# Modulation rows, scratch fills and small weights of later use ordered behind the opening's last modulation row; two more row buffers in the first feed-forward

## The chip, the cores and the metric

The kernel runs on one core of a Trainium2 chip. The metric is the device time of one execution in microseconds (us); a kernel's time is the median of its runs. TensorE (PE) multiplies matrices into PSUM banks, VectorE (DVE) and ScalarE (ACT) work element by element, GpSimd (POOL) does the rest, and SyncE (SP) issues nearly all DMAs of this kernel, in one queue and in the order in which they stand in it. Each engine works through its instructions in order; semaphores make one wait for another.

## What is computed

A decoder trunk of two layers in float32: 256 tokens, model width 2048, feed-forward width 5632. In each layer a vector of 6 x 2048 modulation values comes from the conditioning vector:

```python
cond = jax.nn.silu(c)
for l in range(DEPTH):
    mod = (jnp.einsum('bd,de->be', cond, w_ada[l]) + b_ada[l]).reshape(B, N_MOD, 1, D_MODEL)
    sh_m, sc_m, gt_m, sh_f, sc_f, gt_f = [mod[:, i] for i in range(N_MOD)]
    u = x * (1 + sc_m) + sh_m
    proj = u @ w_in[l]
    ...
    mix = jnp.concatenate([y_attn, y_rwkv], axis=-1) @ w_out[l]
    x = layer_norm(DEEPNORM_ALPHA * x + gt_m * mix, ln1_w[l], ln1_b[l])
    u = x * (1 + sc_f) + sh_f
    gate, up = jnp.split(u @ w_gate_up[l], 2, axis=-1)
    ffn = (jax.nn.silu(gate) * up) @ w_down[l]
    x = layer_norm(DEEPNORM_ALPHA * x + gt_f * ffn, ln2_w[l], ln2_b[l])
```

`y_attn` is sliding-window attention over part of the projected columns and `y_rwkv` a linear recurrence with data-dependent decay over the others. The modulation weights alone are 2 x 2048 x 12288 values, about 200 MB, of which every value is used once.

## The kernel before, in words

**Planning.** The program is written in the order of the mathematics; a planner then fixes the order of the instructions on each engine ahead of time, by a simulated timeline and by the order in which they were written. A tile comes from a pool by a tag with a number of buffers; an instruction that writes a tile waits until the earlier user of that buffer is done. `tc.add_manual_dep(a, b, order, ...)` adds an edge without a semaphore: on their common queue `a` is put behind `b`.

**Modulation rows.** One row is a tile `ast` of 128 x 1024 values, 512 KB of `w_ada`. DVE multiplies row j by the conditioning value `cond[:, j]` and adds it to `aacc`. After 16 rows TensorE transposes the sums, ACT adds them up and DVE writes them to `mods`.

**The opening** (`ada_first`, lines 340 to 356, called by `parts`, line 1354) needs the first two modulation vectors of layer 0 before anything can be projected. It goes by column parts of 4, 4, 4, 2 and 2 blocks of 128 columns (`PARTS`), with eight row buffers, and behind each part the input projection of these columns runs (`front`). Lines 351 and 353 are DVE's sums, line 322 the transposes. `lead` holds the name of the last modulation row's DMA issued so far (line 348). Line 1374 lays later parameter rows behind it through `setup`. Then follow `rope` and the two fills of the DRAM scratch `tinv` with zeros (line 1381), which the inversion in the recurrence later writes partly over (line 790).

**All other modulation values** come in units of 1024 columns, 16 rows each, by `ada_steps` (line 251), which runs as a side stream: `pump` (line 378) advances it by `pace` steps per weight tile. Its rows (line 261) have two buffers in the pool `adap`. The first product is line 263, the other sums line 265, and these are laid behind the weight stream by `anchor`. In part of the mixer of layer 0 the flag `direct` sends rows through TensorE instead (`ada_direct`).

**Weights** are fetched by `steps` (line 414): a raw tile of 128 x 1024 with four buffers (line 422), which ACT rounds to a high part `hi` (line 430) and DVE subtracts to a low part `lo` (line 431). `stream` and `tstream` multiply both parts (lines 452 to 455 and 464 to 466).

**Decays** (line 640) loads for each group of heads two small weights into the tile `w2a2` (lines 644 and 645).

**The feed-forward** in `channel` (line 1180, pool `fp`) goes over eleven blocks of 512 gate and 512 up columns, in two groups of six and five, each group followed by the down projection of its rows. Line 1283 is the gate's activation, line 1329 the end of a down projection's block.

Of the kernel before, what the change touches and what calls it, by code (L numbers as in the profile page):

```python
# [10 lines left out]
F32 = mybir.dt.float32  # L11
# [8 lines left out]
P = 128  # L20
# [49 lines left out]
def hybrid_trunk_kernel(  # L70
# [9 lines left out]
    dma = nc.sync.dma_start  # L80
# [4 lines left out]
    adap = ctx.enter_context(tc.tile_pool(name="adap", bufs=1))  # L85
# [6 lines left out]
    def bank(name="mb", tag="mb"):  # L92

        if tag == "cb":
            return ps.tile([P, 512], F32, tag="cb", name=name)
        t = f"m{turn[0]}"
        turn[0] ^= turn[1]
        return ps.tile([P, 512], F32, tag=t, name=name, bufs=1)
# [49 lines left out]
    order = mybir.DependencyInfo(mybir.DependencyClass.NoSync, mybir.DependencyReason.DATA)  # L148
# [20 lines left out]
    def drv(l, nm, i, n=1):  # L169
        return der[l][:, DO[nm] + i:DO[nm] + i + n]  # L170

    def setup(sp, l, half, behind=None):

        prow = sp.tile([P, P], F32, tag="prow", bufs=2, name=f"prow{l}{half}")
        G.memset(prow, 0.0)
        lst = [[("b_ada", b_ada[l], 96), ("ln1_w", ln1_w[l], 16), ("ln1_b", ln1_b[l], 16)],
               [("ln2_w", ln2_w[l], 16), ("ln2_b", ln2_b[l], 16), ("w0", rwkv_w0[l], 8),
                ("a0", rwkv_a0[l], 8), ("k_k", rwkv_k_k[l], 8), ("k_a", rwkv_k_a[l], 8),
                ("r_k", rwkv_r_k[l].rearrange("h d -> (h d)"), 8), ("gn_w", rwkv_gn_w[l], 8),
                ("gn_b", rwkv_gn_b[l], 8), ("mu", rwkv_mu[l, 0:26 * P], 26)]][half]  # L180

        def load(dst, src):
            ins = dma(dst, src)
            if behind:
                tc.add_manual_dep(ins.ins, behind[0], order, reason="behind the first modulation rows")

        r = 0
        for nm, src, n in lst:
            load(prow[r:r + n], src.rearrange("(r q) -> r q", q=P))
            PC[nm] = half * P + r  # L190
            r += n
            yield
        if half:
            load(prow[r:r + 1, 0:32], rwkv_mu[l:l + 1, 26 * P:26 * P + 32])
            r += 1
            PC["v0"] = P + r
            if l > 0:
                load(prow[r:r + 8], rwkv_v0[l - 1].rearrange("(r q) -> r q", q=P))
            load(nsink[l], attn_sinks[l:l + 1, :].to_broadcast([P, 16]))
            V.tensor_scalar_mul(nsink[l], nsink[l], -1.0)  # L200
            yield
        pt = bank()
        PE.transpose(pt[:, 0:P], prow, ident)
        V.tensor_copy(par[l][:, half, :], pt[:, 0:P])
        if half:
            V.tensor_scalar(drv(l, "omu", 0, 27), prm(l, "mu", 0, 27), -1.0, 1.0, ALU.mult, ALU.add)
            V.tensor_scalar_mul(drv(l, "w0h", 0, 8), prm(l, "w0", 0, 8), 0.5)
            V.tensor_scalar_mul(drv(l, "a0h", 0, 8), prm(l, "a0", 0, 8), 0.5)
            V.tensor_scalar_mul(drv(l, "kah", 0, 8), prm(l, "k_a", 0, 8), 0.5)
            V.tensor_scalar(drv(l, "okah", 0, 8), prm(l, "k_a", 0, 8), -0.5, 1.0, ALU.mult, ALU.add)  # L210
            V.tensor_scalar_mul(drv(l, "kkh", 0, 8), prm(l, "k_k", 0, 8), -0.5)
            V.tensor_scalar_mul(drv(l, "v0h", 0, 8), prm(l, "v0", 0, 8), 0.5)
# [38 lines left out]
    def ada_steps(l, mod, c0):  # L251

        src = w_ada[l].rearrange("(j p) n -> p j n", p=P)
        n0 = mod * D + c0
        if direct[0]:
            yield from ada_direct(l, mod, c0, src[:, :, n0:n0 + 1024])
            return
        acc = adap.tile([P, 1024], F32, tag="aacc", name="aacc")
        for j in range(KT):
            t = adap.tile([P, 1024], F32, tag="ast", name="ast", bufs=2)  # L260
            dma(t, src[:, j, n0:n0 + 1024])
            if j == 0:
                V.tensor_scalar_mul(acc, t, cond[:, 0:1])
            else:
                ins = V.scalar_tensor_tensor(acc, t, cond[:, j:j + 1], acc, ALU.mult, ALU.add)  # L265
                if anchor:
                    tc.add_manual_dep(ins.ins, anchor[0], order, reason="behind the weight stream")
            yield
        for _ in range(LAG):
            yield  # L270

        ada_sums(l, mod, c0, [acc[:, i * P:(i + 1) * P] for i in range(8)])
        done.add((l, mod, c0 // 1024))
        yield
# [63 lines left out]
    lead = []  # L338
# [19 lines left out]
    done = set()  # L358
# [14 lines left out]
                       + halves(1, 5))  # L373
    pace = [0.0, 0.0]
    anchor = []
    direct = [False]

    def pump():

# [160 lines left out]
    def mixer(l, us, mixp, feeds):  # L540
# [33 lines left out]
        if l > 0:  # L574
# [7 lines left out]
            for p2 in range(4):  # L582
# [3 lines left out]
                for i in range(2):  # L586
                    p = 2 * p2 + i
                    PE.matmul(b[:, i * T:(i + 1) * T], lhsT=v2t[64:96, i * P:(i + 1) * P], rhs=hv, start=True, stop=True)
                for i in range(2):
                    p = 2 * p2 + i  # L590
# [49 lines left out]
        def decays(g):  # L640

            gsl = slice(g * T, (g + 1) * T)
            w2a2 = pa.tile([P, T], F32, tag="w2a2", name="w2a2", bufs=1)
            dma(w2a2[0:64, :], rwkv_w2[l, :, gsl])
            dma(w2a2[64:128, :], rwkv_a2[l, :, gsl])
            zb, ab = bank("zb"), bank("ab")
            for i in I2:
                PE.matmul(zb[:, i * T:(i + 1) * T], lhsT=w2a2[0:64, i * P:(i + 1) * P], rhs=twd[0:64, :], start=True, stop=True)
                PE.matmul(ab[:, i * T:(i + 1) * T], lhsT=w2a2[64:128, i * P:(i + 1) * P], rhs=xwa[64:128, :],
                          start=True, stop=True)  # L650
            st = [dict(p=2 * g + i) for i in I2]
            for i in I2:
                s_, p = st[i], 2 * g + i
                lw = pa.tile([P, T], F32, tag="t_lw", name="lw", bufs=2)
                S.activation(lw, zb[:, i * T:(i + 1) * T], AF.Tanh, scale=0.5, bias=drv(l, "w0h", p))
                s_["tha"] = tha = pa.tile([P, T], F32, tag="t_tha", name="tha", bufs=4)
                S.activation(tha, ab[:, i * T:(i + 1) * T], AF.Tanh, scale=0.5, bias=drv(l, "a0h", p))
                V.tensor_scalar(lw, lw, -0.5 * DECAY, -0.5 * DECAY, ALU.mult, ALU.add)
                V.tensor_tensor_scan(lw, rmask, lw, 0.0, ALU.mult, ALU.add)
                s_["e1"] = e1 = pa.tile([P, NCH, CH + 1], F32, tag="e1", name="e1", bufs=4)  # L660
                V.memset(e1[:, :, 0:1], 1.0)
                S.activation(e1[:, :, 1:CH + 1], lw.rearrange("p (c s) -> p c s", s=CH), AF.Exp)
                s_["el"] = el = pb.tile([P, NCH, 1], F32, tag="el", name="el", bufs=4)
                S.activation(el, lw.rearrange("p (c s) -> p c s", s=CH)[:, :, CH - 1:CH], AF.Exp)
                s_["e2"] = e2 = pa.tile([P, T], F32, tag="t_e2", name="e2", bufs=4)
                S.activation(e2, lw, AF.Exp, scale=-1.0)
            vt_ = bank("vt")
            if g == 0:
                warm(vt_, IDLE["dec"][l])
            for cc in range(NCH):  # L670
                for i in I2:
                    PE.matmul(vt_[KH[i], cc * P:(cc + 1) * P], lhsT=vx[:, 2 * g + i, cc * CH:(cc + 1) * CH], rhs=cent,
                              start=True, stop=True)
            for i in I2:
                st[i]["uv"] = uv = pb.tile([P, NCH, P], F32, tag="uv", name="uv", bufs=4)
                S.copy(uv[KH[i]].rearrange("p c s -> p (c s)"), vt_[KH[i]])
            return st
# [396 lines left out]
        for op in ORDER[l].split():  # L1074
            n = int(op[1:] or 0)
# [104 lines left out]
    def channel(l, ys, wa, fp):  # L1180
# [31 lines left out]
        for c0, w in ((1024, 512), (1536, 512)):  # L1212
            nq = w // 512
            bk = all_banks(nq)
            src, pieces = cols(w_out[l], c0, w), [(q * 512, 512) for q in range(nq)]
            kts, held = list(range(KT)), None
            apart = SPLIT_O[l] if c0 == 1536 else 0
            n = KT - apart
# [39 lines left out]
                dma(out[0, t * P:(t + 1) * P, o:o + 512], zq)  # L1258

        gtf = fp.tile([P, D], F32, tag="gt", name="gtf")  # L1260
        wg = w_gate_up[l].rearrange("(k p) (s n) -> p k s n", p=P, s=2)
        first = True
        for lo_g, hi_g in ((0, 6), (6, 11)):
            hts = []
            for f in range(lo_g, hi_g):
# [3 lines left out]
                if f == 0:  # L1269
# [4 lines left out]
                    rows = affine()  # L1274
# [31 lines left out]
            for c0, w in ((0, 1024), (1024, 512), (1536, 512)):  # L1306
# [3 lines left out]
                if apart:  # L1310

                    n = len(kts) - 16
# [5 lines left out]
                for ts in ((0,), (1,)) if apart else ((0, 1),):  # L1318
# [5 lines left out]
                    for t in ts:  # L1324
# [8 lines left out]
                        if c0 == 1536 and not first:  # L1333
                            finish(t) if l + 1 == L else normalise(fp, z, t, stt[t])
            first = False
        if l + 1 == L:
            return None, None
        us = []
# [12 lines left out]
    with tc.tile_pool(name="pro", bufs=1) as pp:  # L1351
        xv = x[0].rearrange("(t p) d -> p t d", p=P)

        def parts():
            k0 = 0
            for n in PARTS:
                o, w = k0 * P, n * P
                xt = pp.tile([P, 2, 512], F32, tag="xt", name="xt", bufs=2)[:, :, 0:w]
                side = setup(pp, 0, 0) if k0 == 0 else iter(())
                rows = ada_first(pp, o, w)  # L1360
# [17 lines left out]
            zt = pp.tile([P, 520], F32, name="zt")  # L1378
            G.memset(zt, 0.0)
            for t in tinv:  # L1380
                dma(t.rearrange("e s t -> (e s t)").rearrange("(p n) -> p n", p=P), zt)
        feeds = front(0, us, parts(), ahead=True)
    for l in range(L):
        pace[0] = AP[l]
# [35 lines left out]
```

## Time and profile before

| | us |
|---|---|
| median of 3 runs | 2670.3 |
| lowest and highest run | 2658.5 and 2673.1 |
| the profiled execution | 2673.2 |
| its span, first to last instruction | 2671.2 |
| PE busy in it | 2514.0 |
| DVE busy in it | 1804.7 |
| ACT busy in it | 1186.5 |

The profile is of one execution. Its views are: the page with the span in 40 slices and the chain of work that ended last; groups of instructions by line; waits (who waited for whom: total us, times, longest); the timeline; and windows, which give each engine's busy time in a stretch with the number of its instructions, the clock granted to TensorE, the busy share of the DMA engines and GB/s. "L265" is line 265 of the kernel. "ast<-in_w_ada_dram" is a DMA from the modulation weights into a row tile, "SPq" the queue of SP. An engine's idle time matters only where the end of the program waits for it.

### The profile page before, as it was taken

Reading aid. Unit: us, or ns where it says so; the run is one execution under the profiler, and the core shown is the slowest. Engines: PE = TensorE matmul, PEld = TensorE weight load, DVE = VectorE, ACT = ScalarE, POOL = GpSimd, SP = SyncE. Lnnn points to the kernel's source line nnn. Section 1 sums busy time; section 2 is a strip of 40 time slices with the busy share of each in tenths; the row PEclk is TensorE's granted clock in tenths of the full one; section 3 lists DMA queues with packets and bytes.
Section 4 is the critical chain, followed back from the end, with each engine's and each line's share of the span. In section 5 each row is a group of like instructions: output and inputs, shape, how many; then the busy total and the mean of one; then the engine's idle time right before and its main releaser. Section 6 shows DMA issues by size and latency. Waiting matters only on the chain.

```text
span 2671.2 us, 42267 instructions
## 1 busy us (share of the span) xinstructions
PE 2514.0 (94%) x15619; PEld 2090.1 (78%) x15619; DVE 1804.7 (68%) x2439; ACT 1186.5 (44%) x2023; POOL 146.7 (5%) x368
## 2 busy tenths in 40 slices
PE   3799998999999999999999998989899999999997
PEld 3697785677878888888788977867788888888887
DVE  7977766579877777677787776564855455545456
ACT  2464454435544444444454644543444443344442
POOL 1002212000000000000000024110000000000000
PEclk9899998999999999999999999988999999999999
DMA  9978658698998889888878785414655655566654
GB/s 371 358 215 253 202 176 266 207 335 301 327 328 303 309 301 317 284 299 304 293 247 291 218 264 148 129 50 179 221 189 184 195 184 196 195 190 188 191 189 149
DMA packets 336384, 637.51 MB, mean 239 GB/s; under 512 B 59510, under 2 KB 126514, under 8 KB 334642
## 3 DMA queue, kind: packets, MB, share of 16 engines
q1 hardware_dynamic: 333170, 629.05, 71.0%
q0 software_dynamic: 1280, 2.62, 0.4%
q10 hardware_dynamic: 1728, 3.15, 0.3%
q8 instruction: 122, 2.00, 0.3%
q14 instruction: 84, 0.69, 0.1%
HBM read 622.08 MB, written 12.62 MB: 238 GB/s over the span
## 4 chain that ended last, share of the span: by engine, by line
PE 62%; DMA 6%; DVE 5%; ACT 1%; issue 1%; POOL 0%; SPq 0%; DVEq 0%; ACTq 0%; POOLq 0%
PE acc L453 18%; PE acc L455 17%; PE acc L452 17%; DMA ast<-in_w_ada_dram 3%; DVE lo L431 2%; PE acc L465 1%; PE acc L466 1%; PE acc L464 1%; DMA raw<-in_w_gate_up_dram 1%; DVE aacc L265 1%; PE mb L1290 1%; DMA raw<-in_w_out_dram 1%; DMA raw<-in_w_in_dram 1%; PE mb L322 0%; DMA tm<-tinv 0%
## 5 line engine op out<-in xcount | busy, mean ns | idle before, releaser
L430 ACT CAST hi<-raw 128x1024 fp32r<-128x1024 f32 (+2 forms) x728 | 758.2, 1044 | 1093.2 <-PE acc L455 826.5
L431 DVE TENSOR_TENSOR lo<-raw,hi 128x1024 fp32r<-128x1024 f32 (+2 forms) x728 | 880.4, 1212 | 519.0 <-PE acc L453 350.1
L453 PE MATMUL acc<-lo,u 128*128 128x512 f32 x1568 | 515.7, 396 | 14.3 <-DVE lo L431 14.3
L455 PE MATMUL acc<-hi,u 128*128 128x512 f32 x1568 | 508.1, 392 | 0.0
L452 PE MATMUL acc<-hi,u 128*128 128x512 f32 x1568 | 460.1, 395 | 0.7 <-ACT u L410 0.7
L265 DVE SCALAR_TENSOR_TENSOR aacc<-ast,cond,aacc 128x1024 f32<-128x1024 f32 x270 | 345.7, 1280 | 105.8 <-DMA ast<-in_w_ada_dram 104.5
L453 PEld LDWEIGHTS acc<-lo,u 128*128 128x128 f32 x1568 | 294.2, 189 | 80.2 <-DVE lo L431 20.1
L452 PEld LDWEIGHTS acc<-hi,u 128*128 128x128 f32 x1568 | 296.3, 189 | 63.3 <-issue 1.2
L455 PEld LDWEIGHTS acc<-hi,u 128*128 128x128 f32 x1568 | 296.3, 189 | 61.9 <-issue 0.3
L453 PE MATMUL acc<-lo,ht 128*128 128x512 f32 (+1 forms) x720 | 243.7, 377 | 3.4 <-DVE lo L431 3.0
L455 PE MATMUL acc<-hi,ht 128*128 128x512 f32 (+1 forms) x720 | 242.2, 375 | 0.0
L452 PE MATMUL acc<-hi,ht 128*128 128x512 f32 (+1 forms) x720 | 217.1, 376 | 0.0
L464 PE MATMUL acc<-u,hi 128*128 128x256 f32 x720 | 201.1, 287 | 1.8 <-ACT hi L430 1.8
L465 PE MATMUL acc<-u,hi 128*128 128x256 f32 x720 | 201.3, 287 | 0.0
L466 PE MATMUL acc<-u,lo 128*128 128x256 f32 x720 | 188.7, 289 | 1.9 <-DVE lo L431 1.7
L453 PEld LDWEIGHTS acc<-lo,ht 128*128 128x128 f32 x720 | 135.1, 188 | 30.2 <-DVE lo L431 6.4
L455 PEld LDWEIGHTS acc<-hi,ht 128*128 128x128 f32 x720 | 135.6, 188 | 24.2
L452 PEld LDWEIGHTS acc<-hi,ht 128*128 128x128 f32 x720 | 134.8, 188 | 24.4
L464 PEld LDWEIGHTS acc<-u,hi 128*128 128x128 f32 x720 | 139.8, 194 | 4.5 <-ACT hi L430 2.0
L465 PEld LDWEIGHTS acc<-u,hi 128*128 128x128 f32 x720 | 139.6, 194 | 2.9 <-issue 1.6
L466 PEld LDWEIGHTS acc<-u,lo 128*128 128x128 f32 x720 | 130.7, 194 | 6.5 <-DVE lo L431 3.3
L1130 POOL TENSOR_TENSOR brs<-brs,mhalf 128x1 f32<-128x1 f32 x8 | 7.3, 916 | 1711.9 <-DVE brs L1129 776.6
(358 smaller groups left out, 2923.6 us busy)
## 6 DMA issues: line engine op xcount, KB each, us to landing
ast<-in_w_ada_dram SPq DMA_DIRECT2D x368, 512.0 KB
raw<-in_w_gate_up_dram SPq DMA_DIRECT2D x704, 256.0 KB
raw<-in_w_down_dram SPq DMA_DIRECT2D x176, 512.0 KB
raw<-in_w_in_dram SPq DMA_DIRECT2D x82, 512.0 KB
raw<-in_w_out_dram SPq DMA_DIRECT2D x64, 512.0 KB
raw<-in_w_in_dram SPq DMA_DIRECT2D x120, 256.0 KB
ast<-in_w_ada_dram SPq DMA_DIRECT2D x32, 256.0 KB
lnw<-in_ln_w_dram SPq DMA_DIRECT2D x4, 1024.0 KB
```

What stands on the lines that cost most here:

```text
L265: ins = V.scalar_tensor_tensor(acc, t, cond[:, j:j + 1], acc, ALU.mult, ALU.add)
L430: S.copy(h, fl)
L431: ins = V.tensor_tensor(r, fl, h.bitcast(F32), ALU.subtract)
L452: PE.matmul(bt, lhsT=xh, rhs=hi[:, c0:c0 + w], start=st, stop=False)
L453: PE.matmul(bt, lhsT=xh, rhs=lo[:, c0:c0 + w], start=False, stop=False)
L455: PE.matmul(banks[t][q][:, 0:w], lhsT=xl, rhs=hi[:, c0:c0 + w], start=False, stop=sp_)
L464: PE.matmul(bt, lhsT=hi[:, c0:c0 + w], rhs=xh, start=st and opens, stop=False)
L465: PE.matmul(bt, lhsT=hi[:, c0:c0 + w], rhs=xl, start=False, stop=False)
L466: PE.matmul(bt, lhsT=lo[:, c0:c0 + w], rhs=xh, start=False, stop=sp_ and closes)
L1130: G.tensor_tensor(rs[:, 0:1], rs[:, 0:1], mhalf[:, 0:1], ALU.pow)
L1290: PE.transpose(b[:, i * T + t * P:i * T + (t + 1) * P], hh[t][:, (2 * k2 + i) * P:(2 * k2 + i + 1) * P], ident)
```

## The change

A helper `fetch` issues a DMA and, if asked to, lays it behind `lead[0]`, the opening's last modulation row. It is used for the first two rows of the side stream's first unit, for the `w2a2` loads of the first group in layer 0, and for both fills of `tinv`. A list `side` names, while the feed-forward's loops run, two pools from which the side stream's row tiles are taken in turn: even rows from `adap`, odd rows from `fp`, each with two buffers. Outside of them all rows come from `adap`.

```diff
+    def fetch(dst, src, later=True):
+        ins = dma(dst, src)
+        if later:
+            tc.add_manual_dep(ins.ins, lead[0], order, reason="behind the first modulation rows")
+
...
         for j in range(KT):
-            t = adap.tile([P, 1024], F32, tag="ast", name="ast", bufs=2)
-            dma(t, src[:, j, n0:n0 + 1024])
+            t = (side[j % 2:] or [adap])[0].tile([P, 1024], F32, tag="ast", name="ast", bufs=2)
+            fetch(t, src[:, j, n0:n0 + 1024], j < 2 and not done)
...
-    direct = [False]
+    direct, side = [False], []
...
-            dma(w2a2[0:64, :], rwkv_w2[l, :, gsl])
-            dma(w2a2[64:128, :], rwkv_a2[l, :, gsl])
+            fetch(w2a2[0:64, :], rwkv_w2[l, :, gsl], l + g == 0)
+            fetch(w2a2[64:128, :], rwkv_a2[l, :, gsl], l + g == 0)
...
         gtf = fp.tile([P, D], F32, tag="gt", name="gtf")
+        side[:] = [adap, fp]
...
             first = False
+        side.clear()
...
             for t in tinv:
-                dma(t.rearrange("e s t -> (e s t)").rearrange("(p n) -> p n", p=P), zt)
+                fetch(t.rearrange("e s t -> (e s t)").rearrange("(p n) -> p n", p=P), zt)
```

## The prediction

> **What bounds the kernel now.** I read the page first: the span, the chain that ended last, the 40 slices. Then the windows of the two stages that the change touches, and in each the waits of PE, DVE, ACT and SP, to see which wait ends last there.
>
> ```profile
> span 2671.2 us, 42267 instructions
> PE 62%; DMA 6%; DVE 5%; ACT 1%; issue 1%; POOL 0%; SPq 0%; DVEq 0%; ACTq 0%; POOLq 0%
> ```
>
> The chain runs mostly through TensorE. What the change can reach is the small rest: DMA 6% and DVE 5%, and of these only the opening and the first feed-forward.
>
> The opening, by windows (us; busy of PE, PEld, DVE, ACT, POOL; granted clock; DMA share; GB/s):
>
> ```profile
> 0.00:23.00 23.00, 0.70 (x2) 0.36 (x2) 15.07 (x25) 2.42 (x3) 6.91 (x61) 1.00 0.93 331
> 23.00:36.00 13.00, 0.31 (x2) 0.31 (x3) 10.09 (x20) 1.97 (x3) 0.00 (x0) 1.00 1.06 385
> 36.00:50.00 14.00, 9.22 (x47) 7.46 (x45) 8.21 (x13) 7.21 (x27) 0.00 (x0) 1.00 1.04 396
> 50.00:134.00 84.00, 64.20 (x465) 59.97 (x465) 78.54 (x97) 34.62 (x80) 0.00 (x0) 0.89 1.03 365
> 134.00:160.00 26.00, 25.93 (x203) 25.67 (x204) 13.64 (x27) 12.47 (x25) 1.01 (x4) 0.91 0.60 172
> ```
>
> Up to 134 us the DMA share is at or above 1. DVE, which reduces the modulation rows, is free for part of 23 to 50 us (8.7 us idle of 27) and nearly full afterwards (78.54 of 84). From 134 us PE is full and the DMA engines are at 0.60. So the opening passes from DMA to DVE to PE, and time won early is kept only if DVE takes it.
>
> The first feed-forward, against the same stretch of the second one (first gate to last gate activation), which fetches no modulation rows:
>
> ```profile
> 674.00:1263.00 589.00, 584.30 (x2638) 480.92 (x2637) 442.65 (x413) 261.25 (x382) 0.00 (x0) 1.00 0.89 307
> 1971.40:2545.00 573.60, 573.60 (x2570) 475.14 (x2569) 287.52 (x264) 239.43 (x248) 0.00 (x0) 1.00 0.60 191
> ...
> L322 PE MATMUL mb<-ident,aacc 128*128 128x128 f32 x64 | 8.8, 272 | 0.0
> ```
>
> The first takes 589.0 - 573.6 = 15.4 us longer. 8.8 us of it is TensorE's own work on the sums (64 transposes, 8 units of rows at 8 each), which stays; 4.7 us is PE idle (589.0 - 584.3). Over the whole stage, 655 to 1400 us, the waits are these, PE first (total, times, longest):
>
> ```profile
> PE acc L453 <- DVE lo L431: 7.8, 12, 1.7
> ...
> DVE aacc L265 <- DMA ast<-in_w_ada_dram: 65.3, 48, 4.0
> ...
> SPq L261 <- DVE aacc L265: 112.1, 141, 1.7
> ...
> ACT hi L430 <- DMA raw<-in_w_gate_up_dram: 37.4, 18, 5.4
> ```
>
> DVE stands 65.3 us for rows, but PE only 7.8 us for DVE. So 7.8 us caps what deeper row buffers can bring there. SP stands 112.1 us in total until DVE frees a row's buffer: the two buffers are what the row fetches wait for. The chain shows how such a wait gets to PE, with rows and weights late in turn:
>
> ```profile
> 735.95 6.39 DMA ast<-in_w_ada_dram
> 742.39 1.22 DVE lo L431
> 743.63 3.69 DMA raw<-in_w_gate_up_dram
> ```
>
> **The change part by part.** First, what goes behind the opening's last modulation row. SP's queue before, with the last opening rows at its end, and the sizes:
>
> ```profile
> 23.89 0.35 SPq L1381 DMA_DIRECT2D tinv<-zt  x1
> ...
> 25.31 0.34 SPq L1381 DMA_DIRECT2D tinv<-zt  x1
> 26.66 0.56 SPq L644 DMA_DIRECT2D w2a<-in_rwkv_w_dram  x1
> 27.32 0.53 SPq L348 DMA_DIRECT2D ast<-in_w_ada_dram  x1
> 28.39 0.48 SPq L645 DMA_DIRECT2D w2a<-in_rwkv_a_dram  x1
> 29.75 0.83 SPq L261 DMA_DIRECT2D ast<-in_w_ada_dram  x2
> ...
> 41.77 0.34 SPq L261 DMA_DIRECT2D ast<-in_w_ada_dram  x1
> ...
> 120.69 2.58 SPq L348 DMA_DIRECT2D ast<-in_w_ada_dram  x4
> ...
> ast<-in_w_ada_dram SPq DMA_DIRECT2D x368, 512.0 KB
> ...
> tinv<-zt SPq DMA_DIRECT2D x2, 260.0 KB
> w2a<-in_rwkv_w_dram SPq DMA_DIRECT2D x8, 64.0 KB
> w2a<-in_rwkv_a_dram SPq DMA_DIRECT2D x8, 64.0 KB
> ```
>
> Two scratch fills, two small weight loads and two rows (L261) are ordered behind the last row. The third row (41.77 us) is not named by the edit, but it needs the buffer of the first one, so it goes along. Bytes: 2 x 260 + 2 x 64 + 3 x 512 = 2184 KB, 2.24 MB; at the window's 385 GB/s that is 5.8 us of DMA time taken out of 23 to 45 us, where the share is above 1. SP's issue time for them (0.35 + 0.34 + 0.56 + 0.48 + 0.83 + 0.34 = 2.9 us) goes along, and is in that.
>
> How much of 5.8 us does DVE take? Its waits from 23 to 50 us:
>
> ```profile
> DVE aacc L353 <- DMA ast<-in_w_ada_dram: 3.1, 3, 1.8
> DVE u L411 <- ACT u L410: 2.8, 3, 1.9
> DVE mods L329 <- ACT mb L326: 1.8, 1, 1.8
> DVE aacc L351 <- DMA ast<-in_w_ada_dram: 0.4, 1, 0.4
> ```
>
> 3.1 + 0.4 = 3.5 us is for rows and should go. The other 4.6 us is for ACT, and goes only if earlier rows are put into these gaps in DVE's fixed order. Ends: 0 (what comes next is late instead) and 5.8 (all the DMA time). I take 4, near the 3.5 that a row names. From 50 to 134 us DVE is full, so a gain made before stays a gain; the opening's end on PE has room for it:
>
> ```profile
> PE mb L322 <- DVE aacc L353: 4.3, 1, 4.3
> ```
>
> That is PE's wait for the last rows at 130 to 134 us; if they come 4 us earlier, this wait goes and PE's work is late next.
>
> Where the moved transfers land: behind 123 us SP still issues the small parameter rows and the projection weights. The window from 134 to 160 us has 0.60 of the DMA engines busy, 10 us free, which hides 5.8 us. Behind the moved ones on SP stand the projection weights (L422), and for these wait ACT, DVE and PE. The consumers come late enough, each first row below being the earliest of its kind:
>
> ```profile
> 165.55 0.81 ACT L657 ACTIVATE tha<-ab,der 128x256 f32<-128x256 f32 x2
> ...
> 178.18 1.28 DVE L265 SCALAR_TENSOR_TENSOR aacc<-ast,cond,aacc 128x1024 f32<-128x1024 f32 x1
> ...
> L790 POOL DMA_DIRECT2D tinv<-ttl x16: 687/715/908, 232.5 to 1745.2; - x16
> ```
>
> The two small loads feed the matmul just ahead of 165.55 us, the rows (but for the first one's product, for which nobody waits) the sum at 178.18, the fills the stores at 232.5. Cost taken: 0. If that cover is gone, up to 5.8 us comes back.
>
> Second, the two buffers. While the feed-forward runs, odd rows of a unit go to a second pair of buffers, so four rows may be under way in place of two. No instruction is added or removed; every row is 512 KB as before. The fetch of a row no longer waits for the row two before it, and SP's stands on L261 shrink, with the weights behind them. Ends: 0 (the rows wait for bandwidth, share 0.89) and 7.8 us. The chain's lines show both causes, rows waiting for a buffer and weights for bandwidth, so I take a little under half, 3.5 us. The second feed-forward has no rows left:
>
> ```profile
> L261 SPq DMA_DIRECT2D ast<-in_w_ada_dram x288: 327/328/1997, 29.7 to 1612.8; - x144
> ```
>
> The last row is issued at 1612.8 us, so nothing changes there. The new pair takes space that the mixer had before and gives it back to the next one; the trace has no row for waits on that, and I bound it by the longest wait of PE at that change of stage, 1.6 us either way, and take 0:
>
> ```profile
> PE mb L404 <- DVE z L1141: 1.6, 1, 1.6
> ```
>
>
> Sum: -4 - 3.5 = -7.5 us. The profiled execution took 2673.2 us (span 2671.2 and 2 us around it), so 2665.7 in its terms; the median of the three runs is 2.9 us lower, 2670.3, so 2662.8, rounded to 2663.
>
> In 674 to 1263 us PE is busy 584.30 of 589.00, and DVE 442.65. [...]
>
> **The rivals.** (a) Given back: the moved 2.24 MB stands in SP's queue ahead of the projection weights of the last column parts. For it:
>
> ```profile
> ACT hi L430 <- DMA raw<-in_w_in_dram: 4.9, 2, 3.5
> ```
>
> From 120 to 140 us ACT already waits for such weights. Against it: those weights come earlier in the program. Then the opening brings about 0; and if the rows of the feed-forward wait for bandwidth too, that term is 0. One or both: 2666 to 2671, I take 2668. That the edits do nothing ends in the same place.
>
> (b) More: DVE's order takes up all 5.8 us, and all of 7.8 us goes: 2670.3 - 13.6 = 2656.7.
>
> (c) Slower: at the start of each unit four rows are issued at once where two were, and a weight tile issued behind them comes 2 x 512 KB later, at 385 GB/s 2.7 us. It decides from the point where the weights' lead is below 2.7 us; ACT's 37.4 us of waits for weights in this stage says that the lead is gone 18 times. With the 8 units of the quoted window at 2.7 us, and the opening's 4 us kept: 2670.3 + 21.6 - 4 = 2688. Against it: PE has taken ACT's 37.4 us with only 7.8 us of its own waits. The Trainium skill, in DMA: Bandwidth & Descriptors, section Queues, rings and completion order, says that each DMA engine consumes descriptors in ring order; by that rule the rows in front do delay the weight behind them, and no row of this trace gives a landing time for it.
>
> **How the numbers follow.** Forecast 0.48, (a) 0.28, (b) 0.18, (c) 0.06. The time is the forecast's, 2663. Beside these the new ordering edges may shift the order on the engines elsewhere, some us either way, and the three runs shown spread from 2658.5 to 2673.1. Bounds: 2670.3 - 13.6 less some scatter, and (a) with its own; 2651 to 2675 leaves out (c) and the edges, some 2 in 10. A measurement of this kernel tells about 0.5%, 13.4 us, from no change. Faster by more: over half of (b) and the forecast's edge, 0.17. Slower by more: (c), 0.06. Within: 0.77.
>
> **What would show it.** Right: no L1381, L644 or L261 issue before the last L348; DVE's row waits from 23 to 50 us gone; PE's last wait for L353 under 4.3 us; the opening's PE work over some 4 us earlier; DVE's row waits in the feed-forward far below 65.3 us, PE's below 5 us and the gate-to-gate stretch near 585 us. Wrong: ACT's waits for L422 grown at 120 to 140 us (a); row waits gone with PE's 7.8 us unchanged (a); ACT's waits for weights above 37.4 us with PE's waits grown at the units' starts (c).

## The result, and the profile after

| | before | after |
|---|---|---|
| median, us | 2661.5 (6 runs, 2658.2 to 2673.1) | 2645.6 (6 runs, 2641.7 to 2651.0) |
| the profiled execution, us | 2673.2 | 2641.7 |
| its span, us | 2671.2 | 2640.0 |

The ratio of the times is 0.9931, with a 95% interval of 0.9917 to 0.9946. By the medians the change brings 15.9 us where 7.5 was forecast, by the ratio 0.69%, and 2645.6 lies below the range. The direction was right, the size not: no change beyond 0.5% was the likeliest outcome in the prediction, and it is faster by more. About half of the distance to the predicted 2663 is no matter of the change: it started from 2670.3, the median of three runs, and with six runs before stands at 2661.5.

In the changed kernel most lines are some five further down, and every DMA that goes through `fetch` has line 173: row sums are L268 and L270 (were L263 and L265), the opening's row sum L358 (L353), `hi` and `lo` L435 and L436 (L430 and L431), raw weights L427 (L422), matmuls L457 to L460 (L452 to L455).

The profiled executions differ by 31.2 us, twice what the medians do. So I cut the span into stages at the same instructions of each trace and set beside both a second profile of either program (e1 and e4 below). The cuts: first scan of a mixer (L664), its last output product (L1233), the feed-forward's first gate (L1289), its last down product (L1335).

| stage, us | before | e1, same program | after | e4, same program | difference of means |
|---|---|---|---|---|---|
| opening, to the first scan | 168.8 | 168.5 | 163.3 | 164.3 | -4.9 |
| mixer of layer 0 | 441.9 | 439.9 | 437.6 | 452.4 | +4.1 |
| its layer norm, to the first gate | 63.3 | 62.8 | 61.7 | 59.8 | -2.3 |
| first feed-forward, to the last down product | 708.4 | 705.2 | 698.3 | 698.2 | -8.6 |
| to the first scan of layer 1 | 112.9 | 112.9 | 112.7 | 112.6 | -0.3 |
| mixer of layer 1 | 419.6 | 411.2 | 410.7 | 407.5 | -6.3 |
| the rest | 756.4 | 756.2 | 755.9 | 756.4 | -0.2 |

Two stages differ clearly by more than the same program differs from itself: the opening and the first feed-forward, 13.5 us together. The layer norm is 2.3 us shorter by the means, but the changed kernel differs from itself there by 1.9, so I don't count it. The mixers scatter with the clock that was granted. The mixer of layer 0, by the windows of the changed kernel's two profiles (length, busy of PE, PEld, DVE, ACT, POOL, granted clock, DMA share, GB/s), first the one and then the other:

```profile
163.27:600.88 437.61, 410.45 (x3706) 326.63 (x3706) 309.38 (x546) 200.69 (x449) 62.83 (x146) 0.97 0.76 249
```

```profile
164.32:616.69 452.37, 422.12 (x3710) 334.84 (x3709) 310.33 (x546) 200.85 (x449) 62.41 (x146) 0.94 0.74 241
```

One program, and 14.8 us between two executions of one stage; of these 11.7 are PE's busy time at clocks of 0.97 and 0.94. DVE and ACT work as long in both. A difference between two single profiles says nothing here unless the stage and its clock are looked at.

**The opening.** The windows of before, cut at the end of DVE's last sum of opening rows:

```profile
23.00:50.00 27.00, 9.53 (x47) 7.77 (x47) 18.30 (x32) 9.19 (x29) 0.00 (x0) 1.00 1.05 391
50.00:133.90 83.90, 64.20 (x465) 59.97 (x465) 78.44 (x97) 34.52 (x80) 0.00 (x0) 0.89 1.03 365
```

and of after:

```profile
23.00:50.00 27.00, 10.29 (x53) 8.53 (x54) 21.19 (x35) 9.15 (x29) 0.00 (x0) 1.00 1.05 391
50.00:128.06 78.06, 60.58 (x461) 56.69 (x459) 73.84 (x93) 33.41 (x79) 0.00 (x0) 0.91 1.03 363
```

The last sum ends 5.84 us earlier. The DMA engines run at the same 391 GB/s as before; what changed is what they carry. DVE's third column shows where it came from: idle before 50 us fell from 8.70 to 5.81 (-2.89), idle behind 50 us from 5.46 to 4.22 (-1.24), and DVE's work ahead of the last sum by 1.71. DVE's waits from 23 to 50 us in the changed kernel (total, times, longest):

```profile
DVE aacc L358 <- DMA ast<-in_w_ada_dram: 2.5, 2, 1.9
DVE u L416 <- ACT u L415: 1.9, 3, 0.9
DVE mods L334 <- ACT mb L331: 0.9, 1, 0.9
```

The row waits did not go, 3.5 became 2.5; the waits for ACT fell from 4.6 to 2.8.

Not all of it reaches the first scan. By the means of the two profiles of each program the last sum comes 6.1 us earlier and the first scan 4.9; from the one to the other it takes 35.7 us in place of 34.5. PE is not idle longer there (0.9 and 1.8 us, against 1.3 and 1.5 in the kernel before and e1) but busy longer: 34.3 and 34.4 us against 33.6 and 32.6, at granted clocks of 0.89 and 0.88 against 0.89 and 0.92.

**The first feed-forward**, first gate to last down product, by windows; before:

```profile
674.03:1382.40 708.37, 701.28 (x3272) 581.20 (x3271) 538.01 (x523) 312.32 (x471) 0.54 (x1) 1.00 0.89 306
```

and after:

```profile
662.57:1360.84 698.27, 696.05 (x3261) 580.26 (x3262) 539.23 (x525) 314.09 (x477) 0.54 (x1) 1.00 0.88 310
```

PE's idle time fell from 7.09 to 2.22 us, and its busy time by 5.23 at an unchanged clock of 1.00. In e1, the program before once more, the idle time was 4.59 and the stage 705.2, so the gain from single profiles is uncertain by some 3 us. The waits of after in the same stage as the prediction showed of before (shifted to 643 to 1378 us), one fence for each engine; PE:

```profile
PE acc L458 <- DVE lo L436: 1.6, 2, 1.0
PE acc L457 <- ACT sg L1289: 1.2, 1, 1.2
```

DVE, the longest, and then the first of these lines in the kernel before:

```profile
DVE lo L436 <- PE acc L458: 81.8, 56, 2.3
DVE lo L436 <- issue: 53.0, 109, 2.6
```

```profile
DVE lo L431 <- PE acc L453: 48.5, 36, 2.3
```

ACT and SP:

```profile
ACT hi L435 <- DMA raw<-in_w_gate_up_dram: 29.0, 14, 4.4
```

```profile
SPq L173 <- DVE aacc L270: 75.1, 131, 1.6
```

No line with a row's DMA is left among DVE's waits; it was 65.3 us. DVE now waits 81.8 us for PE (48.5 before): PE is the last to arrive more often. SP stands 75.1 us for row buffers in place of 112.1, and ACT waits less for weights too, 29.0 in place of 37.4.

### The profile page after: what moved, and what is told of

Its sections match the earlier page's. It is cut to its first block, busy times and chain, and to the rows that moved or that the text cites. A ratio compares the mean times of both kernels' runs of the same rounds, so it can differ in the third digit from the quotient of the medians.

```text
span 2640.0 us, 42213 instructions
## 1 busy us (share of the span) xinstructions
PE 2499.2 (95%) x15619; PEld 2081.6 (79%) x15619; DVE 1803.9 (68%) x2439; ACT 1185.9 (45%) x2023; POOL 144.1 (5%) x368
## 4 chain that ended last, share of the span: by engine, by line
PE 80%; DMA 10%; DVE 7%; issue 2%; ACT 1%; SPq 0%; POOL 0%; DVEq 0%; ACTq 0%; POOLq 0%
PE acc L458 21%; PE acc L457 20%; PE acc L460 20%; DMA ast<-in_w_ada_dram 5%; PE acc L471 2%; PE acc L469 2%; PE acc L470 2%; DVE lo L436 2%; DMA raw<-in_w_in_dram 1%; DVE aacc L270 1%; DMA raw<-in_w_out_dram 1%; DVE aacc L358 1%; PE mb L1296 1%; PE mb L327 1%; PE gv L290 1%
## 5 line engine op out<-in xcount | busy, mean ns | idle before, releaser
L436 DVE TENSOR_TENSOR lo<-raw,hi 128x1024 fp32r<-128x1024 f32 (+2 forms) x728 | 881.3, 1211 | 556.7 <-PE acc L458 378.2
L435 ACT CAST hi<-raw 128x1024 fp32r<-128x1024 f32 (+2 forms) x728 | 758.2, 1044 | 1051.8 <-PE acc L460 831.0
L460 PE MATMUL acc<-hi,u 128*128 128x512 f32 x1568 | 508.1, 393 | 0.0
L457 PE MATMUL acc<-hi,u 128*128 128x512 f32 x1568 | 460.0, 395 | 2.0 <-ACT sg L1289 1.2
L270 DVE SCALAR_TENSOR_TENSOR aacc<-ast,cond,aacc 128x1024 f32<-128x1024 f32 x270 | 344.9, 1277 | 39.5 <-DMA ast<-in_w_ada_dram 39.0
L457 PEld LDWEIGHTS acc<-hi,u 128*128 128x128 f32 x1568 | 296.1, 189 | 65.1 <-ACT sg L1289 1.6
L460 PEld LDWEIGHTS acc<-hi,u 128*128 128x128 f32 x1568 | 296.7, 189 | 61.7
L460 PE MATMUL acc<-hi,ht 128*128 128x512 f32 (+1 forms) x720 | 242.2, 375 | 0.0
L457 PE MATMUL acc<-hi,ht 128*128 128x512 f32 (+1 forms) x720 | 217.0, 376 | 0.0
L460 PEld LDWEIGHTS acc<-hi,ht 128*128 128x128 f32 x720 | 135.6, 188 | 24.3
L457 PEld LDWEIGHTS acc<-hi,ht 128*128 128x128 f32 x720 | 134.8, 188 | 24.3
```

Source lines behind the costliest of these rows:

```text
L435: S.copy(h, fl)
L436: ins = V.tensor_tensor(r, fl, h.bitcast(F32), ALU.subtract)
L457: PE.matmul(bt, lhsT=xh, rhs=hi[:, c0:c0 + w], start=st, stop=False)
L460: PE.matmul(banks[t][q][:, 0:w], lhsT=xl, rhs=hi[:, c0:c0 + w], start=False, stop=sp_)
```

## The experiments

All edits are to the changed kernel. Each ratio is to the kernel before, run on the same chip beside it.

**First set: neither part, each part alone, both.** e1 takes both parts out and is the kernel before again:

```diff
-        if later:
+        if later and False:
...
-        side[:] = [adap, fp]
+        side[:] = []
```

> Neither part: rows, fills and small loads are not laid behind the last modulation row, and no second pair of row buffers is used; the program is that of before. Every theory: ratio to before 1.000 within 0.002. It shows how far two executions of the same program lie apart stage by stage. Theory S (8 us of the 31 us between the two profiled executions, those at the second layer's output projection, are scatter between executions): from the second layer's last score reduction to the end of its output projection this run lies anywhere from 109 to 118 us. Theory C (those 8 us come from the change): 117 us or more, as in the profile of before (117.4).

e2 has only the second of these edits (the order stays), e3 only the first (the buffers stay), e4 is the changed kernel.

> The ordering behind the last modulation row alone, without the second pair of row buffers. Theory A (the two parts add: the opening takes all 5.8 us of DMA time and keeps it, the rest is the buffers'): 5 to 7 us faster than before, ratio 0.9975 to 0.998; last opening row at about 128 us, first gate activation of the first feed-forward 6 us earlier than before's 674. Theory M (the ordering also shortens the mixer of the first layer, through another order of its instructions): 9 to 12 us faster, ratio 0.9955 to 0.9965, first gate activation 10 to 12 us earlier. First feed-forward, gate activation to gate activation: 589 us as before under both.

> The second pair of row buffers alone, without the ordering. Theory A: 9 to 11 us faster than before, ratio 0.996 to 0.9965; last opening row at 134 us as before; gate to gate 582 us in place of 589, and 3 us more by the end of the first feed-forward. Theory M: 5 to 7 us faster, ratio 0.9975 to 0.998, by the same stretch.

> The changed kernel once more, for a second profile. Every theory: ratio 0.993 within 0.0015. Theory S: the stretch from the second layer's last score reduction to the end of its output projection differs from the 109 us of the first profile of this kernel by several us. Theory C: 109 us again, within 1 us.

| | median, us | ratio | 95% |
|---|---|---|---|
| e1 neither | 2665.1 | 1.0003 | 0.9987 to 1.0019 |
| e2 only the order | 2679.6 | 1.0055 | 1.0035 to 1.0074 |
| e3 only the buffers | 2656.9 | 0.9975 | 0.9963 to 0.9986 |
| e4 both | 2644.5 | 0.9937 | 0.9914 to 0.9959 |

The parts do not add up: the order alone costs half a per cent, where both theories expected a gain, and on top of the buffers it brings 0.4%. For e3 the feed-forward came out as the first theory had it, the total as the second. By stages, though, each part acts where the prediction put it. The opening's last sum ends at 128.12 us in e2 and 134.77 in e3 (134.46 in e1); the feed-forward takes 708.7 us in e2 and 698.6 in e3 (705.2 in e1). What does not add up lies in stages that neither edit touches: in e2 the mixer of layer 1 takes 427.9 us (407 to 420 in the other three and before), and in e3 the layer norm ahead of the feed-forward has a longer wait than in e1.

e1 and e4 were also to show whether the change shortens the second layer's output projection. From the last score reduction to the last output product it takes 117.4 us before and 113.5 in e1, 109.2 in the changed kernel and 108.8 in e4. The program before scatters there by 3.9 us, so that question stays open.

First the wait, in PE's waits of e3 from the last score reduction (L989) to the first gate:

```profile
PE mb L409 <- DVE z L1146: 9.0, 1, 9.0
```

e1 has 3.4 us there, the changed kernel 2.5. The whole stage is 64.2 us long in e3, 62.8 in e1, 61.7 and 59.8 in the changed kernel, so not all of the 9.0 us is loss. What DVE does meanwhile, from the timeline of e3 (start, length, engine, line, operation; in brackets the idle time ahead and what ended it):

```profile
616.05 0.54 DVE L1146 TENSOR_SCALAR z<-z,brs 128x512 f32<-128x512 f32 x1
...
617.53 1.28 DVE L270 SCALAR_TENSOR_TENSOR aacc<-ast,cond,aacc 128x1024 f32<-128x1024 f32 x1 [0.35 <-DMA ast<-in_w_ada_dram]
...
620.16 1.28 DVE L270 SCALAR_TENSOR_TENSOR aacc<-ast,cond,aacc 128x1024 f32<-128x1024 f32 x1 [0.74 <-DMA ast<-in_w_ada_dram]
...
622.71 1.28 DVE L270 SCALAR_TENSOR_TENSOR aacc<-ast,cond,aacc 128x1024 f32<-128x1024 f32 x1 [0.90 <-DMA ast<-in_w_ada_dram]
...
624.02 1.28 DVE L270 SCALAR_TENSOR_TENSOR aacc<-ast,cond,aacc 128x1024 f32<-128x1024 f32 x1
625.23 1.00 DVE L1146 TENSOR_SCALAR z<-z,brs 128x512 f32<-128x512 f32 x2
```

Four row sums stand in DVE's fixed order between the first block's normalisation (616.05) and the second's (625.23), three of them waiting for their rows. In the changed kernel the same two steps stand 2.2 us apart with one sum between:

```profile
604.59 1.01 DVE L1146 TENSOR_SCALAR z<-z,brs 128x512 f32<-128x512 f32 x2
...
605.59 1.27 DVE L270 SCALAR_TENSOR_TENSOR aacc<-ast,cond,aacc 128x1024 f32<-128x1024 f32 x1
606.78 0.99 DVE L1146 TENSOR_SCALAR z<-z,brs 128x512 f32<-128x512 f32 x2
```

So the planner's order can move a step by microseconds in a stage that the edit does not touch. The next set asks whether it explains e2.

**Second set: what of the order costs, and how many buffers it takes.** e5 defers the rows alone, without the buffers (fills and `w2a2` not deferred):

```diff
-            fetch(w2a2[0:64, :], rwkv_w2[l, :, gsl], l + g == 0)
-            fetch(w2a2[64:128, :], rwkv_a2[l, :, gsl], l + g == 0)
+            fetch(w2a2[0:64, :], rwkv_w2[l, :, gsl], False)
+            fetch(w2a2[64:128, :], rwkv_a2[l, :, gsl], False)
...
-        side[:] = [adap, fp]
+        side[:] = []
...
-                fetch(t.rearrange("e s t -> (e s t)").rearrange("(p n) -> p n", p=P), zt)
+                fetch(t.rearrange("e s t -> (e s t)").rearrange("(p n) -> p n", p=P), zt, False)
```

> Of the ordering, the two modulation rows alone (the third follows them); fills and small loads where they were; no second pair of buffers. In this program the order of the instructions in the second layer's mixer is that of before on every engine, which it is not in the run with the whole ordering alone. Theory P (the ordering is worth its 5 to 6 us in the opening, and the run with the ordering alone lost 15 to 20 us because the planner came to another order in the second layer's mixer): 3 to 7 us faster than before, ratio 0.9975 to 0.999; last opening row 3 to 6 us earlier. Rival Q (the rows and fills cost more at their new place than they freed, through the first layer's mixer): slower than before, ratio 1.003 or more.

e6 changes nothing in the opening and keeps two row buffers, but takes them from the other pool:

```diff
-        if later:
+        if later and False:
...
-        side[:] = [adap, fp]
+        side[:] = [fp, fp]
```

> No ordering; in the first feed-forward all rows come from the new pair of buffers alone, so two rows are under way as before. By chance of the planner the second layer's mixer has in this program, on every engine, the order that it has in the run with the ordering alone. Theory P: opening and first feed-forward as before (last opening row 134 us; 705 to 709 us from the first gate activation to the end of the down projection), the second layer's mixer and output projection 15 to 20 us longer (425 to 430 us from its first scan in place of 408 to 420), ratio 1.005 to 1.0075. Rival Q: as before throughout, ratio 1.000 within 0.002.

e7 is e5 with the change's buffers. e8 is the whole change with one buffer of odd rows in place of two:

```diff
-... name="ast", bufs=2)
+... name="ast", bufs=1 if side and j % 2 else 2)
```

> The second pair of buffers, and of the ordering the rows alone. Here the second layer's mixer has for the most part the order of the run with the ordering alone. Theory P: opening 3 to 6 us and feed-forward 9 us better, mixer 15 to 20 us worse: 1 to 6 us slower than before, ratio 1.0005 to 1.0025. Rival Q: between the buffers alone and the whole change, ratio 0.9935 to 0.9975.

> The whole change with one more row buffer in the feed-forward in place of two (three under way). Theory D (a row's wait for its buffer is what costs, and one more buffer covers most of it): first gate activation to the end of the down projection 699 to 702 us, against 707 with two and 698 with four; ratio 0.993 to 0.9945. Rival B (four are needed): 703 to 707 us, ratio 0.995 to 0.997.

| | median, us | ratio | 95% |
|---|---|---|---|
| e5 rows deferred | 2666.1 | 1.0023 | 1.0009 to 1.0037 |
| e6 other pool, same depth | 2683.1 | 1.0085 | 1.0068 to 1.0103 |
| e7 rows deferred, four buffers | 2671.2 | 1.0033 | 1.0015 to 1.0051 |
| e8 whole, three buffers | 2646.0 | 0.9943 | 0.9925 to 0.9960 |

e6 is the clean case: nothing is moved in the opening and no more rows are under way, and it is 0.85% slower. In e6 and e2 the planner gave PE the same order in the mixer of layer 1, line for line, and another than in e1 from about the first third on; e7's is nearly theirs. In all other kernels the order there is e1's but for some late instructions. Those three take 423 to 430 us for this mixer, the others 407 to 411, but for the one profile of the kernel before with 420. From the first scan to the last score reduction PE is idle for 26.3, 26.4 and 27.9 us in e2, e6 and e7, and for 16.9 to 22.5 in all others. The windows of this stretch, and PE's largest waits there, in e6 (two fences):

```profile
1498.73:1810.22 311.49, 285.12 (x2821) 236.12 (x2821) 204.23 (x397) 149.10 (x354) 60.83 (x145) 0.93 0.53 159
```

```profile
PE acc L458 <- DVE lo L436: 5.2, 3, 3.5
PE ob L868 <- ACT state L887: 4.1, 1, 4.1
PE db L878 <- DVE rh L857: 3.9, 2, 2.9
```

and in e1:

```profile
1489.23:1786.91 297.68, 279.95 (x2863) 233.40 (x2861) 205.81 (x404) 147.61 (x350) 64.84 (x145) 0.95 0.55 166
```

13.8 us longer, of which 8.6 is PE's idle time (26.37 against 17.73), in many short waits along the recurrence and the scores; the other 5.2 is busy time at a granted clock of 0.93 in place of 0.95. Against the kernel before, e2 and e6 have no edit in common, only this order. So what e2 loses here is an order of instructions, not traffic of the opening. e7 loses it too and comes out a little slower than expected, e5 between its two expectations.

e8 shows the depth: DVE's and PE's waits in its feed-forward, first gate to last down product, are

```profile
DVE aacc L270 <- DMA ast<-in_w_ada_dram: 36.1, 28, 2.2
```

```profile
PE acc L458 <- DVE lo L436: 2.3, 3, 1.0
```

DVE still waits 36.1 us for rows, but PE no more than with four, and the stage takes 700.2 us against 698.3. The third buffer brings most of it, as the first theory for e8 had it.

e5 shows a second loss. Its last opening sum ends at 129.27 us, 5.2 ahead of e1, but its first scan is at 170.21, behind e1's 168.49. SP's timeline of e5 around the deferred rows:

```profile
132.32 0.91 SPq L173 DMA_DIRECT2D ast<-in_w_ada_dram  x2
133.33 2.00 SPq L427 DMA_DIRECT2D raw<-in_w_in_dram  x2
140.71 0.33 SPq L173 DMA_DIRECT2D ast<-in_w_ada_dram  x1
141.41 1.72 SPq L427 DMA_DIRECT2D raw<-in_w_in_dram  x3
```

and of the changed kernel:

```profile
129.81 0.94 SPq L173 DMA_DIRECT2D tinv<-zt  x2
...
132.19 1.06 SPq L173 DMA_DIRECT2D ast<-in_w_ada_dram  x2
133.34 1.90 SPq L427 DMA_DIRECT2D raw<-in_w_in_dram  x3
137.65 0.33 SPq L173 DMA_DIRECT2D ast<-in_w_ada_dram  x1
```

The third row needs the first one's buffer. SP stands at it from 135.3 to 140.7 us in e5, with the opening's last weights behind it, and from 135.2 to 137.7 in the changed kernel. DVE in e5 meanwhile:

```profile
138.63 0.17 DVE L205 TENSOR_SCALAR nsink<-nsink 128x16 f32<-128x16 f32 x1 [5.73 <-DMA nsink<-in_attn_sinks_dram]
139.93 0.75 DVE L268 TENSOR_SCALAR aacc<-ast,cond 128x1024 f32<-128x1024 f32 x1 [1.13 <-DMA ast<-in_w_ada_dram]
140.60 1.62 DVE L436 TENSOR_TENSOR lo<-raw,hi 128x576 fp32r<-128x576 f32 x2
```

DVE, too, stands: 5.73 us for a small parameter row and 1.13 for the first row's product, with the `lo` of the opening's weights behind both. And for this `lo` PE waits, and ACT for the raw weights (118 to 170 us):

```profile
PE lb L471 <- DVE lo L436: 4.1, 1, 4.1
```

```profile
ACT hi L435 <- DMA raw<-in_w_in_dram: 15.0, 4, 7.5
```

In the changed kernel ACT waits 8.2 us for these weights, e1 3.9, and PE has no such wait for their `lo` in either.

PE's wait costs more than its 4.1 us. The windows of e5 behind it, from its end on:

```profile
141.40:146.80 5.40, 5.40 (x25) 5.22 (x26) 2.04 (x2) 2.73 (x6) 0.00 (x0) 0.50 0.78 247
146.80:152.00 5.20, 5.20 (x48) 5.20 (x47) 2.15 (x3) 1.61 (x3) 0.00 (x0) 0.99 0.51 133
```

For 5.4 us the granted clock is 0.50, and PE gets through 25 matmuls where it then does 48 in 5.2 us; by the clock that is some 2.7 us more (an estimate from these rows). Together that is the loss: from the last sum to the first scan e5 takes 6.9 us longer than e1, 3.9 of it idle time of PE and 3.0 busy time. The same half clock follows PE's wait for the last rows, before (133.9 to 138.7 us) and after (128.2 to 133.7).

**Third set: the rows behind the opening's last weights.** If the rows' place ahead of the weights is what e5 loses, rows laid behind these weights keep the opening's gain. `raws` holds the last raw weight issued:

```diff
+            tc.add_manual_dep(ins.ins, (later if type(later) is list else lead)[0], order, ...)
...
-            fetch(t, src[:, j, n0:n0 + 1024], j < 2 and not done)
+            fetch(t, src[:, j, n0:n0 + 1024], j < 2 and not done and raws)
...
-                dma(dst, src)
+                raws[:] = [dma(dst, src).ins.name]
```

e9 is e5 with this edit. e10 is e2 with it: the whole order, no buffers. e11 is the whole change with it. e12 defers fills and `w2a2`, but not the rows, and has the buffers:

```diff
-            fetch(t, src[:, j, n0:n0 + 1024], j < 2 and not done)
+            fetch(t, src[:, j, n0:n0 + 1024], False)
```

> As the run with the ordering of the rows alone, but the rows are laid behind the first projection weights of the mixer in place of the last modulation row, so no weight of the opening stands behind them in SP's queue. The second layer's mixer has the order of before but for a few matmuls of the output projection. Theory H (that run lost its gain because SP stood 5 us at the third row, which waits for the first one's buffer, with the opening's weights behind it): last opening row at 129 us, from it to the first scan 34 to 36 us in place of 40.9; 3 to 6 us faster than before, ratio 0.9975 to 0.999. Rival (the rows cost at any later place, by bandwidth): from the last row to the first scan 39 us or more, ratio 1.001 or more.

> The whole ordering, the rows behind the first projection weights of the mixer, no second pair of buffers. Here the second layer's mixer keeps the order of before but for a few matmuls of the output projection, which it did not in the run with the ordering alone (ratio 1.0055). Theory P with H: first scan at 162 to 165 us against 168.5, second layer's mixer 405 to 420 us against 427.9; 4 to 7 us faster than before, ratio 0.9973 to 0.9985. Rival Q (fills and small loads at the new place cost in the first layer's mixer): ratio 1.003 or more.

> The whole change with the rows behind the first projection weights of the mixer. Theory P with H: as the whole change or up to 3 us faster, ratio 0.992 to 0.994, opening to the first scan 162 to 164 us, first gate activation to the end of the down projection 698 us. Rival: slower than the whole change, ratio 0.995 or more.

> The buffers, and of the ordering the fills and small loads alone; the rows stay where they were. The second layer's mixer keeps the order of before. Fills and small loads are 648 of 2184 KB, 1.7 us at 385 GB/s. If the opening's gain goes by bytes: last opening row at 132 to 133 us, 8 to 12 us faster than before in all, ratio 0.9955 to 0.997. If it is the rows' alone: 134 us, ratio as the buffers alone, 0.9975. If the fills are what stood before the first part's last rows: 130 us or less, ratio 0.994.

| | last opening sum, us | first scan, us | feed-forward, us | median, us | ratio | 95% |
|---|---|---|---|---|---|---|
| e9 | 129.31 | 164.11 | 706.9 | 2662.1 | 1.0005 | 0.9990 to 1.0021 |
| e10 | 129.70 | 164.65 | 707.0 | 2653.4 | 0.9969 | 0.9957 to 0.9981 |
| e11 | 128.43 | 163.40 | 698.6 | 2652.5 | 0.9964 | 0.9951 to 0.9977 |
| e12 | 134.71 | 168.26 | 698.5 | 2655.8 | 0.9973 | 0.9960 to 0.9986 |

In the stage it is so: last sum to first scan takes 34.8 us in e9, 40.9 in e5 and 34.0 in e1. Whether SP's stand or DVE's was the larger share, e9 doesn't tell, since both go with the rows. e12 against the others shows that the opening's gain is that of the rows: with fills and small weights deferred alone, the last sum ends no earlier than in e1.

e9's total brings nothing all the same, where 0.1 to 0.25% was expected. The mixer of layer 0 from the first scan to the last score reduction, in e9 and then in e10, by windows:

```profile
164.11:498.58 334.47, 303.82 (x3040) 246.61 (x3042) 224.35 (x420) 150.63 (x350) 65.78 (x145) 0.93 0.71 220
```

```profile
164.65:486.52 321.87, 298.53 (x3023) 242.56 (x3026) 223.38 (x420) 151.41 (x353) 63.62 (x145) 0.94 0.73 226
```

PE is idle 30.65 us in e9, 23.34 in e10 and 21.5 in the changed kernel. PE's order in this mixer is another than e1's in e9, nearly that of e5 and e7, and in e10 almost e1's. The change has a third one and loses nothing, so another order needn't cost. e5 and e7 are idle for 24.0 and 26.4 us there, so the order may explain a part of e9's loss; the rest stays open. e10 is the order part with the mixers' order left nearly as it was: there it brings 0.31%, where it cost 0.55% in e2. e3, e11 and e12 have the layer norm's wait of 9.0, 9.4 and 9.2 us, the changed kernel, e4 and e8 not. e11 was expected to be level with the whole change or a little faster, and is slower; e12 comes out as expected if the opening's gain is the rows' alone. No version beats the whole change; e8 with three buffers is level with it.

## Why the prediction was wrong, step by step

- **What bounds the kernel, and the direction**: right. The gain lies where the two windows put it, and PE, 95% busy now in place of 94%, takes it.
- **The opening's term, 4 of at most 5.8 us**: right mechanism, sized a little too small. The last sum came 5.8 us earlier in this profile (4.8 to 6.4 in the kernels that defer the rows, against e1's), the first scan 4.9 by the means. The step that failed here is the count of DVE's waits: I counted the 3.5 us that name a row and left out the 4.6 for ACT. The row waits fell by only 1.0, those for ACT by 1.8; and behind 50 us, where I called DVE full, 1.2 more went.
- **PE's last wait for the rows**: wrong. It did not go; from 128 us it is still

```profile
PE mb L327 <- DVE aacc L358: 3.9, 1, 3.9
```

  PE's work ahead of it ended 5.5 us earlier (124.29 in place of 129.77 us), so that no room was used up there.
- **Moved transfers hidden, cost 0; rival (a)**: nearly right. By the means 1.2 us of 6.1 did not reach the first scan, and the sign that I had named for (a) showed: from 120 to 140 us ACT's waits for the opening's weights grew from 4.9 to 8.2. PE has no wait for their `lo`, so the cover held, but it was thinner than I had it. I compared bytes with free bandwidth. What hurts, in e5, is a queue: the third row, waiting for a buffer, holds the weights behind it, an order on DVE holds their `lo`, and PE's granted clock is 0.50 behind its wait. Rival (a) was named for the right transfers and the wrong reason. In the changed kernel the first row's product stands at 136.87 us and SP's stand is 2.4 us long, and no wait of PE comes of it.
- **The feed-forward's term, 3.5 of at most 7.8 us**: the largest error, and the step that failed. It brought 8.6 us by the means (e3, e11 and e12 agree with 698.5 to 698.6), more than the end that I called a cap. PE's waits for `lo` fell from 7.8 to 1.6 us, close to what rival (b) had. The rest is busy time, 5.2 us less. The cap was wrong because a wait costs more than the idle time that is shown for it. In before's timeline of PE four matmuls up to a wait, a pair just behind it and the next such pair are

```profile
741.68 1.07 PE L452 MATMUL acc<-hi,u 128*128 128x512 f32 x4
743.65 0.73 PE L453 MATMUL acc<-lo,u 128*128 128x512 f32 x2 [0.91 <-DVE lo L431]
...
744.69 0.62 PE L453 MATMUL acc<-lo,u 128*128 128x512 f32 x2
```

  The pair behind the wait is 0.11 us longer. And a matmul's record is 0.39 us long while the next one begins 0.23 us after it in a dense run; the last one ahead of a wait counts with all of its 0.39, 0.16 us more. With about 11 waits fewer that makes some 1.2 and 1.8 us (estimates from these rows). A further 1.1 us is no work of this stage: at its end, where only DVE's last product is left, fill matmuls that belong to the next layer norm (L107) begin inside the cut, six in before and one in after:

```profile
L107 PE MATMUL mb<-rmask,ident 128*128 128x256 f32 x6 | 1.5, 378 | 0.0
```

```profile
L107 PE MATMUL mb<-rmask,ident 128*128 128x256 f32 x1 | 0.4, 378 | 0.0
```

  About one us stays open; the ends of matmuls are modelled in these records. The reference stretch of the second layer had said it: 15.4 us longer, 8.8 of it work that stays, so 6.6 to be had from gate to gate, of which 4.7 was idle. I quoted both numbers and took the smaller. Gate to gate came down from 589.0 (587.5 in e1) to 582.2, 6.0 by the means.
- **How full PE was**: the Trainium skill, in Perfetto Trace Analysis, section Identifying the Most-Contended Engine, says that TensorE's busy share is not a good measure of how close it is to its limit. This case's trace agrees: PE was busy 584.30 of 589.00 us from gate to gate, which left 4.7, and 6.0 came out.
- **Weights held back by four rows at a unit's start, rival (c)**: didn't happen. ACT's waits for weights fell from 37.4 to 29.0 us, and PE's with them.
- **The second layer's feed-forward unchanged, the space of the new pair at 0**: right for the former. For the latter I took 1.6 us as the bound, and e6 shows that taking the buffers from the other pool can cost 0.85% by the order that follows from it. "Some us either way" for new orders stood in the text, but the bound was far too narrow: 13.8 us in a part of the mixer of layer 1, a wait of 9.0 us in place of 3.4 in the layer norm. That the change as made has none of these losses is luck; nothing in the working foresaw it.
- **The starting point**: 8.8 us of the miss, as said above.

The two touched stages give 13.5 us, the medians 15.9, and e4's ratio 11 to 23 us. What the remaining few microseconds are stays open; the layer norm's 2.3 may be among them, but e11, with both parts, has none of that. The mixer of layer 1 is 6.3 us shorter by the means, but 411.2 us in e1 and 410.7 in the changed kernel are the same, and the kernel before alone was at 420, so I don't count it to the change.

## What to carry to other kernels

The idle time that a trace shows ahead of the busiest engine is no upper bound on what its waits cost: compare the stage with a like one that has none of them, and take that difference. Behind a wait of some four microseconds look at the granted clock as well. A DMA that must wait for a buffer is placed by what stands behind it in its queue, not by its bytes; look for the first one that has to wait. Where a planner fixes the order, try each part of a change alone and together and compare stage by stage, since an order that flips elsewhere can be worth more than the part itself.

## What I had not expected of the hardware

The same stage of one program took 437.6 and 452.4 us in two executions, with a granted clock of 0.97 and 0.94, while the whole executions had nearly the same mean clock (0.978 and 0.976). The feed-forward with its dense matmuls had 1.00 in all of them; with four buffers it repeats to 0.1 us (698.27 and 698.20), with two it differed by 3.2 (708.4 and 705.2). So the scatter with the clock sits in the mixers, and in the feed-forward a single profile can be trusted to some 3 us, not to tenths.

A wait of 4 us of PE was followed by some 5 us at a granted clock of 0.50, in the opening of the kernel before, of the changed kernel and of e5; the waits of up to 1.7 us in the feed-forward left it at 1.00.
